# A hybrid decoder layer with expert retrieval: the dense expert loop's second stage with 512 moving columns, waits of single tiles, and 44 gathered expert rows traced later

## The chip, the core and the metric

The kernel runs on one core of a Trainium2 chip. Times are device microseconds (us) of one execution, from the first to the last instruction on the core plus what lies around it. Before the change the median of 3 runs is 2199.97 us (2193.77 to 2200.79). One further execution was taken with the profiler; all rows below are from it.

## What is computed

One layer of a decoder serves 512 prompt tokens (with 16 learned tokens in front) and 32 sample tokens, 1024 wide, all in float32. The first half (projection, a recurrence called RWKV-7, windowed attention, an output projection) gives the residual `x`. The second half is the retrieval of experts, and the change is about that part:

```python
def peer(h, lp):                                   # h = rmsnorm(x): [tokens, 1024]
    q = (hb @ w_query).reshape(n, 8, 2, 128)       # 8 heads, two half keys
    s = jnp.einsum('thcd,cnd->thcn', q, sub_keys)  # scores against 2 x 128 keys
    s1, i1 = lax.top_k(s[:, :, 0], 16)
    s2, i2 = lax.top_k(s[:, :, 1], 16)
    top, sel = lax.top_k(s1 + s2 (all 256 pairs), 16)
    idx = i1 * 128 + i2 at sel                     # 128 experts of 16384 for each token
    gate = softmax(top)
    pre = jnp.einsum('td,tkd->tk', hb, eu[idx])    # dot with row u of each expert
    act = gelu(pre) * gate
    return jnp.einsum('tk,tkd->td', act, ev[idx])  # weighted sum of rows v
# x = x + peer(rmsnorm(x)); y = rmsnorm(x) * final_norm_g
```

The expert tables `eu` and `ev` hold 16384 rows of 4 KB each, 64 MB apiece.

## The kernel before, in words

**Two ways to the experts.** The 512 prompt tokens are four tiles of 128. Tiles 0 and 3 and the samples *gather*: for each of the 128 picks (32 for the samples) one indirect DMA, issued by GpSimd (line 1032, `rows` inside `experts`), fetches one table row for each of 128 partitions, 512 KB, into one of five buffers `gat`. VectorE then takes a dot product (rows of `eu`) or adds the weighted row to the sum (rows of `ev`, tiles `x`); all VectorE instructions are recorded under line 126. That makes 256 gathers for a tile and 64 for the samples, 576 in all.

Tiles 1 and 2, 256 tokens, are done *densely*: every one of the 16384 experts is computed for all 256 tokens, and the weights of the experts that a token did not pick are zero. The table is cut into 128 blocks of 128 experts. Each block has these steps:

- `block_in` loads 128 rows of `eu` and of `ev`, transposes the `eu` rows on TensorE, and splits both into a high part in the fp32r format and a low part, the remainder (`uH`, `uL`, `vH`, `vL`; the split of `v` runs on ScalarE and GpSimd, line 1453).
- `block_u` multiplies with the tokens (`dhH`, `dhL`): 24 products of 256 columns (lines 1460 to 1463); then gelu, the gate, and a split of the result into `aH` and `aL`.
- `block_v` adds the block's part of the output into four PSUM tiles `acc`, which stay there through all 128 blocks: for each eighth of the 1024 output columns a slice of `vH` or `vL` is the weight operand and the activations are the moving operand, 256 columns; three products each (high with high, low with high, high with low, lines 1477 to 1479), 24 in all.

The result is transposed (output columns in the partitions, tokens along the row), so at the end `acc` is copied to `oT`, transposed in 16 pieces, added to the residual and normalised (`finish`).

**The stages in time.** In the *front* come the projections, the recurrences (`recur`), the attentions (`attend`) and the selections (`rest`) of all tiles; by 430 us gathers of tile 0 run beside it, and later those of the samples. Its buffers lie in the pools `sb` and `pp`. When it closes, the pools `dn` and `dp` take the same memory. First the normalised tokens come back from DRAM (line 1421, `hscr`), are transposed (1426) and split (`dhH`, `dhL`). Then `gates` builds, in 32 steps, the table of gate values by one-hot compares on VectorE; then comes the dense loop. Tile 3's selection (`late`) and its gathers run beside the dense loop.

**What sets the order.** The gathers are steps of generators in a list `side`; `beside(n)` traces the next n of them (fractions add up). `AHEAD` steps are traced ahead of the gates, then `RATE_G` = 0.8 for each gate step and `RATE_D` = 3 for each dense block; after the last block `beside(1000)` traces what is left. `issue_after` says behind which instruction such a step may be issued. The order on each engine is then fixed, before the kernel runs, by a list scheduler that follows a model of the timeline. Each engine works through its list in order.

A pool's memory that is handed from one pool to the next is guarded by waits: without an argument the first users of the new pool wait until the old pool as a whole is released; with `reuse_waits="tile"` each new tile waits only for the old tiles whose bytes it takes.

Of the kernel before, what the change touches and what calls it, by code (L numbers as in the profile page):

```python
# [11 lines left out]
F32 = mybir.dt.float32  # L12
# [3 lines left out]
OP = mybir.AluOpType  # L16
AX = mybir.AxisListType
PSUM = bass.MemoryType.PSUM
# [14 lines left out]
LAG = 2  # L33
WST = 3
UV = 5
AHEAD = 280
RATE_G = 0.8
RATE_D = 3.0
LATE = 2
# [74 lines left out]
def hymba_step(ctx, tc, x_prompt, x_sample, cache_k, cache_v, state_wkv, state_shift, meta, norm1_g, w_in, mu, w0,  # L114
# [3 lines left out]
    A, G, T, DM = nc.scalar, nc.gpsimd, nc.tensor, nc.sync  # L118
# [11 lines left out]
    V = V()  # L130
    uid = [0]

    def _t(pool, tag, bufs, shape, dt=F32):
        uid[0] += 1
        return pool.tile(list(shape), dt, tag=tag, name=f"{tag}_{uid[0]}", bufs=bufs)
# [13 lines left out]
    fr = ctx.enter_context(ExitStack())  # L149
# [15 lines left out]
    ident = p0.tile([128, 128], F32, name="ident")  # L165
# [79 lines left out]
    def beside(n):  # L245

        due[0] += n
        while side and due[0] >= 1.0:
            due[0] -= 1.0
            if next(side[0], None) is None:  # L250
                side.pop(0)
        due[0] = min(due[0], 1.0)
# [804 lines left out]
    def finish(x2, y, rows, dst, gf, kind="F"):  # L1057

        rms(x2[:rows], y[:rows], rows, gf, kind)
        DM.dma_start(dst, y[:rows])  # L1060

    def final_g(t):
        G.dma_start(t, fin_g.partition_broadcast(128))
        return t
# [96 lines left out]
    with ExitStack() as px:  # L1161
# [36 lines left out]
        def transposed(h, half, rows):  # L1198
            p = jps().rearrange("p (a b) -> p a b", a=4)
            for j in range(4):  # L1200
                k = 4 * half + j
                transpose(p[:, j, 0:rows], h[:rows, k * 128:(k + 1) * 128])
            return p
# [30 lines left out]
        for half in range(2):  # L1234
            p = transposed(hS, half, 72)
# [41 lines left out]
            project(blk, wt, ws, jps(), lambda k: [t[:, k, :] for t in hA], NA, _t(pj, "own", 2, [128, NA]),  # L1277
                    _t(pj, "po", 3, [128, NA]), 0)

    sb = fr.enter_context(tc.tile_pool(name="sb", bufs=1))  # L1280
    pp = fr.enter_context(tc.tile_pool(name="pp", bufs=1, space=PSUM))
    def meta_wkv():
        r = rwkv_prep(40, 16)
        wkv_local(r)
        meta_state(r)
# [119 lines left out]


    ND = 256
    dn = ctx.enter_context(tc.tile_pool(name="dn", bufs=1))
    dp = ctx.enter_context(tc.tile_pool(name="dp", bufs=1, space=PSUM))

    def dt_(tag, bufs, shape, dt=F32):
        return _t(dn, tag, bufs, shape, dt)

    def dps():
        return _t(dp, "w", 4, [128, 512])
# [3 lines left out]
    for i in range(2):  # L1419
        hn = dt_("uv", UV, [128, 2, D])[:, 0]  # L1420
        DM.dma_start(hn, hscr[1 + i])
        for half in range(2):
            p = dps().rearrange("p (a b) -> p a b", a=4)
            for j in range(4):
                k = 4 * half + j
                T.transpose(p[:, j, :], hn[:, 128 * k:128 * k + 128], ident)
            o = hH[:, 4 * half:4 * half + 4, 128 * i:128 * i + 128]
            A.copy(o, p)
            V.tensor_tensor(hL[:, 4 * half:4 * half + 4, 128 * i:128 * i + 128], p, o.bitcast(F32), OP.subtract)

    acc = [dp.tile([128, 2, ND], F32, name=f"acc{c}", bufs=1) for c in range(4)]
    euv = eu[0].rearrange("(i j) d -> i j d", j=128)
    evv = ev[0].rearrange("(i j) d -> i j d", j=128)

# [36 lines left out]

    def block_v(j, x):
        vH, vL, aH, aL = x
        for d in range(8):
            o = acc[d // 2][:, d % 2, :]
            ds_ = slice(128 * d, 128 * d + 128)
            T.matmul(o, vH[:, ds_], aH, start=(j == 0 and d % 2 == 0), stop=False, skip_group_check=True)  # L1477
            T.matmul(o, vH[:, ds_], aL, start=False, stop=False, skip_group_check=True)  # L1478
            T.matmul(o, vL[:, ds_], aH, start=False, stop=(j == 127), skip_group_check=True)  # L1479

    gA, gB = dt_("gA", 1, [128, 32, 128]), dn.tile([128, 64, 128], F32, name="gB")
    sg = [None]
# [69 lines left out]

    for n in range(AHEAD):
        with tc.issue_after(marks[gather_mark[0]]):
# [20 lines left out]
    for j in range(128):  # L1575
        nxt, mark = None, last
        if j < 127:
            nxt, last = block_u(ins.pop(j + 1), gate_of(j + 1))
        if j < 126:
            ins[j + 2], sub = block_in(j + 2)  # L1580
        block_v(j, mid)
        mid = nxt
        for _ in range(LATE):
            next(more, None)
        with tc.issue_after(mark), tc.issue_after(sub):
            beside(RATE_D)
    oT = gB[:, 0:16, :].rearrange("p a b -> p (a b)").rearrange("p (a b) -> p a b", b=ND)
    for c in range(4):
        A.copy(oT[:, 2 * c:2 * c + 2, :], acc[c])
    gfd = final_g(dt_("uv", UV, [128, 2, D])[:, 0])  # L1590
    for i in range(2):
        xy = dt_("uv", UV, [128, 2, D])
        x2, y = xy[:, 0], xy[:, 1]
        DM.dma_start(x2, xscr[1 + i])
        for half in range(2):
            p = dps()
            for q in range(4):
                k = 4 * half + q
                T.transpose(p[:, 128 * q:128 * q + 128], oT[:, k, 128 * i:128 * i + 128], ident)
            xs_ = x2[:, 512 * half:512 * half + 512]  # L1600
            V.tensor_tensor(xs_, xs_, p, OP.add)
        finish(x2, y, 128, y_p[0, 128 * (i + 1):128 * (i + 1) + 128, :], gfd, "E")
    beside(1000)

# [27 lines left out]
```

## Time and profile before

| | profiled execution before |
|---|---|
| device time of this execution | 2204.76 us |
| span on the core | 2203.0 us |
| mean granted clock of TensorE (1 is 2.4 GHz) | 0.867 |
| TensorE busy | 1839.1 us, 83% |
| VectorE busy | 1690.4 us, 77% |
| GpSimd busy | 1249.2 us, 57% |
| ScalarE busy | 867.3 us, 39% |
| moved by all DMA | 569.51 MB, mean 259 GB/s |

In the rows PE is TensorE's products and PEld its loads of weights, DVE is VectorE, ACT ScalarE, POOL GpSimd, SPq the DMA queue of SyncE. A row of the timeline has the start in us, the duration in us, the engine, the line, the operation, output<-inputs by the program's names, the shape and a count; in square brackets stands how long the engine was idle before and what ended that. A row of a table of windows has the stretch in us, its length, the busy time of each engine with the number of instructions, the granted clock, the mean share of the DMA engines that was busy, and GB/s. The gathers' DMA time is not in GpSimd's busy time: that holds only the issuing.

### The profile page before, as it was taken

The numbers are of one execution on the slowest core, as the hardware profiler recorded it, in microseconds if no ns is written. First come the engines' busy times: TensorE is split into PE (matmuls) and PEld (weight loads), VectorE is DVE, ScalarE is ACT, GpSimd is POOL, SyncE is SP. The second block draws the span as 40 slices with busy tenths as digits, with TensorE's granted clock in tenths as the row PEclk, the third lists the DMA queues.
The fourth block names the chain that finished last, engine by engine and source line by source line (L and its number), as shares of the span: only waits on it lengthen the run. The fifth ranks groups of instructions, "written<-read, shape, count | busy, mean of one in ns | idle before, by whom it ended". The sixth has DMA issues, their size and how long they took to land.

```text
span 2203.0 us, 37197 instructions
## 1 busy us (share of the span) xinstructions
PE 1839.1 (83%) x13915; PEld 1716.0 (78%) x13915; DVE 1690.4 (77%) x3393; ACT 867.3 (39%) x1963; POOL 1249.2 (57%) x963
## 2 busy tenths in 40 slices
PE   5899975585759868996547897899999999999996
PEld 5888974473647747886446787899999999999995
DVE  5543436788788788799989879997778787787887
ACT  6554422211224313323169634334444444444443
POOL 0110103878784676565624546867667776767774
PEclk9999996556755659898778999999999999999998
DMA  7532473687786789996757887799899999999995
GB/s 222 157 101 84 122 191 102 208 288 248 230 273 199 231 273 318 285 317 222 243 163 242 299 313 239 270 326 340 334 330 331 342 326 336 335 325 343 325 330 178
DMA packets 310154, 569.51 MB, mean 259 GB/s; under 512 B 32787, under 2 KB 194565, under 8 KB 309830
## 3 DMA queue, kind: packets, MB, share of 16 engines
q0 software_dynamic: 84048, 305.70, 39.7%
q1 hardware_dynamic: 225926, 261.43, 36.6%
q8 instruction: 110, 1.80, 0.3%
q14 instruction: 70, 0.57, 0.1%
HBM read 543.07 MB, written 24.60 MB: 258 GB/s over the span
## 4 chain that ended last, share of the span: by engine, by line
PE 51%; DVE 22%; DMA 10%; issue 9%; POOL 5%; ACT 3%; SPq 0%; DVEq 0%; POOLq 0%; ACTq 0%
DVE gat L126 5%; PE acc L1478 5%; PE w L1460 5%; PE w L1461 5%; PE w L1463 5%; PE acc L1479 5%; PE acc L1477 5%; PE w L1446 4%; POOL gat L1032 4%; DVE x L126 4%; PE pD L218 3%; DMA gat<-in_expert_v_dram,ei 3%; PE ps L218 2%; DMA wst<-in_w_query_dram 2%; DMA gat<-in_expert_u_dram,ei 2%
## 5 line engine op out<-in xcount | busy, mean ns | idle before, releaser
L126 DVE SCALAR_TENSOR_TENSOR x<-gat,act,x 128x1024 f32<-128x1024 f32 x287 | 427.9, 1491 | 24.7 <-DMA gat<-in_expert_v_dram,ei 23.4
L1032 POOL DMA_INDIRECT gat<-in_expert_u_dram,ei x256 | 343.0, 1340 | 158.8 <-DVE pre L126 75.7
L1032 POOL DMA_INDIRECT gat<-in_expert_v_dram,ei x256 | 294.4, 1150 | 193.6 <-DVE x L126 73.1
L1453 POOL TENSOR_TENSOR vL<-uv,vH 128x1024 fp32r<-128x1024 f32 x128 | 322.5, 2519 | 56.1 <-ACT vH L1452 54.3
L1478 PE MATMUL acc<-aL,vH 128*128 128x256 f32 x1024 | 290.7, 289 | 17.2 <-DVE aL L126 17.1
L1479 PE MATMUL acc<-aH,vL 128*128 128x256 f32 x1024 | 289.3, 287 | 0.0
L1477 PE MATMUL acc<-aH,vH 128*128 128x256 f32 x1024 | 280.5, 295 | 5.3 <-ACT aH L1469 5.3
L1460 PE MATMUL w<-dhH,uH 128*128 128x256 f32 x1024 | 252.5, 284 | 0.2 <-ACT lsc L1548 0.2
L1461 PE MATMUL w<-dhL,uH 128*128 128x256 f32 x1024 | 251.6, 283 | 0.0
L126 DVE CUSTOM_DVE_ANT_0 gat<-gat,h 128x1024 f32<-128x1024 f32 x160 | 213.5, 1343 | 49.6 <-DMA gat<-in_expert_u_dram,ei 47.8
L1478 PEld LDWEIGHTS acc<-aL,vH 128*128 128x128 f32 x1024 | 200.6, 196 | 19.3 <-DVE aL L126 19.3
L126 DVE CUSTOM_DVE_ANT_0 gat<-gat,lx 128x1024 f32<-128x1024 f32 x128 | 214.4, 1686 | 0.0
L1452 ACT CAST vH<-uv 128x1024 fp32r<-128x1024 f32 x128 | 134.6, 1051 | 195.7 <-issue 131.8
L1479 PEld LDWEIGHTS acc<-aH,vL 128*128 128x128 f32 x1024 | 200.6, 196 | 0.0
L1460 PEld LDWEIGHTS w<-dhH,uH 128*128 128x128 f32 x1024 | 196.9, 192 | 0.5 <-ACT lsc L1548 0.4
L1461 PEld LDWEIGHTS w<-dhL,uH 128*128 128x128 f32 x1024 | 196.8, 192 | 0.1
L1477 PEld LDWEIGHTS acc<-aH,vH 128*128 128x128 f32 x1024 | 188.0, 193 | 6.0 <-ACT aH L1469 5.9
L126 DVE TENSOR_TENSOR uL<-w,uH 128x512 fp32r<-128x512 f32 x256 | 167.6, 681 | 3.0 <-ACT uH L1448 3.0
L126 DVE TENSOR_TENSOR w<-w,gl 128x128 f32<-128x128 f32 x128 | 50.5, 395 | 143.3 <-ACT w L1464 143.2
L1463 PE MATMUL w<-dhH,uL 128*128 128x256 f32 x1024 | 151.9, 287 | 2.8 <-DVE uL L126 2.8
L1448 ACT CAST uH<-w 128x512 fp32r<-128x512 f32 x256 | 139.1, 592 | 8.4 <-PE w L1446 3.0
L1446 PE MATMUL w<-ident,uv 128*128 128x128 f32 x1024 | 141.4, 273 | 0.0
(575 smaller groups left out, 4113.8 us busy)
## 6 DMA issues: line engine op xcount, KB each, us to landing
uv<-in_expert_u_dram SPq DMA_DIRECT2D x128, 512.0 KB, 4.5
uv<-in_expert_v_dram SPq DMA_DIRECT2D x128, 512.0 KB, 5.9
wst<-in_w_query_dram SPq DMA_DIRECT2D x48, 512.0 KB, 5.5
wst<-in_w_out_dram SPq DMA_DIRECT2D x24, 512.0 KB, 6.9
wst<-in_w_in_dram SPq DMA_DIRECT2D x20, 512.0 KB, 4.4
h2T<-in_w_in_dram SPq DMA_DIRECT2D x20, 512.0 KB, 4.1
gscr<-uv SPq DMA_DIRECT2D x10, 1024.0 KB, 6.5
gl<-gscr SPq DMA_DIRECT2D x16, 512.0 KB, 7.4
```

Of the source, the lines that this page charges most:

```text
L126: r = getattr(nc.vector, name)(*args, **kw)
L1032: G.indirect_dma_start(out=r, out_offset=None, in_=w[0], in_offset=bass.IndirectOffsetOnAxis(ap=ei[:, k:k + 1], axis=0))
L1446: T.transpose(p[:, q, :], un[:, 128 * k:128 * k + 128], ident)
L1448: A.copy(uH[:, ks, :], p)
L1452: A.copy(vH, vn)
L1453: G.tensor_tensor(vL, vn, vH.bitcast(F32), OP.subtract)
L1460: T.matmul(pre, uH[:, k, :], hH[:, k, :], start=(k == 0), stop=False)
L1461: T.matmul(pre, uH[:, k, :], hL[:, k, :], start=False, stop=False)
L1463: T.matmul(pre, uL[:, k, :], hH[:, k, :], start=False, stop=(k == 7))
L1477: T.matmul(o, vH[:, ds_], aH, start=(j == 0 and d % 2 == 0), stop=False, skip_group_check=True)
L1478: T.matmul(o, vH[:, ds_], aL, start=False, stop=False, skip_group_check=True)
L1479: T.matmul(o, vL[:, ds_], aH, start=False, stop=(j == 127), skip_group_check=True)
```

## The change

The edit has three parts. `AHEAD` is 236 instead of 280, so 44 gather steps that were traced ahead of the gates are traced beside gates and dense blocks. The pools `sb`, `pp`, `dn` and `dp` get `reuse_waits="tile"`. And `block_v` swaps its operands: a slice of 128 tokens of `aH` or `aL` is the weight operand, and 512 columns of `vH` or `vL` move; for each of three pairs, two halves of the tokens and two halves of the columns that makes 12 products. `acc` then holds tokens in the partitions, and the copies to `oT` and the transposes at the end are dropped.

```diff
-AHEAD = 280
+AHEAD = 236
...
-    sb = fr.enter_context(tc.tile_pool(name="sb", bufs=1))
-    pp = fr.enter_context(tc.tile_pool(name="pp", bufs=1, space=PSUM))
+    sb = fr.enter_context(tc.tile_pool(name="sb", bufs=1, reuse_waits="tile"))
+    pp = fr.enter_context(tc.tile_pool(name="pp", bufs=1, space=PSUM, reuse_waits="tile"))
...
-    dn = ctx.enter_context(tc.tile_pool(name="dn", bufs=1))
-    dp = ctx.enter_context(tc.tile_pool(name="dp", bufs=1, space=PSUM))
+    dn = ctx.enter_context(tc.tile_pool(name="dn", bufs=1, reuse_waits="tile"))
+    dp = ctx.enter_context(tc.tile_pool(name="dp", bufs=1, space=PSUM, reuse_waits="tile"))
...
-    acc = [dp.tile([128, 2, ND], F32, name=f"acc{c}", bufs=1) for c in range(4)]
+    acc = [dp.tile([128, 512], F32, name=f"acc{c}", bufs=1) for c in range(4)]
...
     def block_v(j, x):
         vH, vL, aH, aL = x
-        for d in range(8):
-            o = acc[d // 2][:, d % 2, :]
-            ds_ = slice(128 * d, 128 * d + 128)
-            T.matmul(o, vH[:, ds_], aH, start=(j == 0 and d % 2 == 0), stop=False, skip_group_check=True)
-            T.matmul(o, vH[:, ds_], aL, start=False, stop=False, skip_group_check=True)
-            T.matmul(o, vL[:, ds_], aH, start=False, stop=(j == 127), skip_group_check=True)
+        for n, (a, v) in enumerate(((aH, vH), (aH, vL), (aL, vH))):
+            for i in range(2):
+                for c in range(2):
+                    T.matmul(acc[2 * i + c], a[:, 128 * i:128 * i + 128], v[:, 512 * c:512 * c + 512],
+                             start=(j == 0 and n == 0), stop=(j == 127 and n == 2))
...
-    oT = gB[:, 0:16, :].rearrange("p a b -> p (a b)").rearrange("p (a b) -> p a b", b=ND)
-    for c in range(4):
-        A.copy(oT[:, 2 * c:2 * c + 2, :], acc[c])
...
         for half in range(2):
-            p = dps()
-            for q in range(4):
-                k = 4 * half + q
-                T.transpose(p[:, 128 * q:128 * q + 128], oT[:, k, 128 * i:128 * i + 128], ident)
             xs_ = x2[:, 512 * half:512 * half + 512]
-            V.tensor_tensor(xs_, xs_, p, OP.add)
+            V.tensor_tensor(xs_, xs_, acc[2 * i + half], OP.add)
```

**What moves on GpSimd, at the end.** GpSimd's list before, from the last but one dense block's split of `v` (`vL`) on; `gat` rows are gathers of tile 3, and the load of `final_norm_g` belongs to that tile's output.

```order
L1453 TENSOR_TENSOR vL_21325<-uv_21305,vH_21324 128x1024
L1032 DMA gat_18624<-in_expert_v_dram,ei_11_105 128x1024
L1032 DMA gat_18627<-in_expert_v_dram,ei_11_105 128x1024
L1032 DMA gat_18709<-in_expert_v_dram,ei_11_105 128x1024
L1453 TENSOR_TENSOR vL_21404<-uv_21384,vH_21403 128x1024
L1032 DMA gat_18712<-in_expert_v_dram,ei_11_105 128x1024
L1032 DMA gat_18715<-in_expert_v_dram,ei_11_105 128x1024
L1063 DMA gat_18800<-in_final_norm_g_dram 128x1024
```

The same place now:

```order
L1453 TENSOR_TENSOR vL_19837<-uv_19817,vH_19836 128x1024
L1032 DMA gat_17260<-in_expert_v_dram,ei_11_105 128x1024
L1032 DMA gat_17330<-in_expert_v_dram,ei_11_105 128x1024
L1032 DMA gat_17333<-in_expert_v_dram,ei_11_105 128x1024
L1453 TENSOR_TENSOR vL_19904<-uv_19884,vH_19903 128x1024
L1032 DMA gat_17336<-in_expert_v_dram,ei_11_105 128x1024
L1032 DMA gat_17406<-in_expert_v_dram,ei_11_105 128x1024
...
L1032 DMA gat_18550<-in_expert_v_dram,ei_11_105 128x1024
L1032 DMA gat_18553<-in_expert_v_dram,ei_11_105 128x1024
L1063 DMA gat_18559<-in_final_norm_g_dram 128x1024
```

Behind the last block's split stand 2 gathers before and 48 now (of which four are shown). Ahead of the first block's split stand 306 before and 261 now, and between the first and the last split 268 and 267.

**What moves on VectorE, late in the front.** The list before, in the selections of the second tile of the dense part (`MAX`, `hl`, `dsel`); the `ISA` rows on `gat` and `pre` are the dots of gathered rows, and `ax<-pC,sD` are the last two steps of the attention of tile 3.

```order
L126 TENSOR_TENSOR ax_7785<-pC_7947,sD_7938 128x128
L126 TENSOR_TENSOR ax_7785<-pC_7960,sD_7938 128x128
L126 MAX vals_7107<-sco_1488_7046 128x8
L126 ISA gat_8871,pre_8833<-gat_8871,h_1981_8828 128x1024
L126 ISA pre_8833 128x1
L126 TENSOR_TENSOR dsel_18_112<-dsel_18_112,sR_7042 128x32
L126 MAX vals_7107<-sco_1488_7046 128x8 x2
L126 TENSOR_REDUCE dsel_16_110<-ce_7031 128x32
L126 ISA gat_8874,pre_8833<-gat_8874,h_1981_8828 128x1024
```

In the changed list no row of a gather stands in this stretch; the attention's last steps stand at its very end, behind the last selection and just ahead of the dense part's first split (`dhL`):

```order
L126 TENSOR_TENSOR ce_7301<-iota_86,hl_7291 128x512
L126 TENSOR_SCALAR sD_7927<-sD_7924 128x4
L126 TENSOR_TENSOR sD_7934<-sD_7927,snk 128x4
L126 TENSOR_REDUCE dsel_17_111<-ce_7301 128x32
L126 TENSOR_TENSOR sD_7929<-sD_7929,sD_7934 128x4
L126 RECIPROCAL sD_7938<-sD_7929 128x4
L126 TENSOR_TENSOR ax_7785<-pC_7947,sD_7938 128x128
L126 TENSOR_TENSOR ax_7785<-pC_7960,sD_7938 128x128
L126 TENSOR_TENSOR dhL<-w_8003,dhH 128x4x128
L126 TENSOR_TENSOR dhL<-w_8010,dhH 128x4x128
```

The attention of tile 3 moved back by more than 80 instructions, and VectorE has nothing between it and the dense part.

**What moves on TensorE, in a dense block.** The first six products of one block's second stage before (moving operand first, then the weights), of 24:

```order
L1477 MATMUL acc_8033<-aH_9994,vH_9928 128x256
L1478 MATMUL acc_8033<-aL_9995,vH_9928 128x256
L1479 MATMUL acc_8033<-aH_9994,vL_9929 128x256
L1477 MATMUL acc_8033<-aH_9994,vH_9928 128x256
L1478 MATMUL acc_8033<-aL_9995,vH_9928 128x256
L1479 MATMUL acc_8033<-aH_9994,vL_9929 128x256
```

The whole second stage of a block now:

```order
L1477 MATMUL acc_8033<-vH_9792,aH_9858 128x512
L1477 MATMUL acc_8034<-vH_9792,aH_9858 128x512
L1477 MATMUL acc_8035<-vH_9792,aH_9858 128x512
L1477 MATMUL acc_8036<-vH_9792,aH_9858 128x512
L1477 MATMUL acc_8033<-vL_9793,aH_9858 128x512
L1477 MATMUL acc_8034<-vL_9793,aH_9858 128x512
L1477 MATMUL acc_8035<-vL_9793,aH_9858 128x512
L1477 MATMUL acc_8036<-vL_9793,aH_9858 128x512
L1477 MATMUL acc_8033<-vH_9792,aL_9859 128x512
L1477 MATMUL acc_8034<-vH_9792,aL_9859 128x512
L1477 MATMUL acc_8035<-vH_9792,aL_9859 128x512
L1477 MATMUL acc_8036<-vH_9792,aL_9859 128x512
```

Twelve products stand where 24 stood; the low part of the activations, `aL`, is read by the ninth product and not by the second.

## Rows read from the trace of the kernel before

**Rows 1.** The page's head: the span, and busy time of each engine.

```profile
span 2203.0 us, 37197 instructions
...
PE 1839.1 (83%) x13915; PEld 1716.0 (78%) x13915; DVE 1690.4 (77%) x3393; ACT 867.3 (39%) x1963; POOL 1249.2 (57%) x963
```

**Rows 2.** Table of windows: stretch, its length, busy time (instructions) of each engine.

```profile
core 0: us, PE busy (x) PEld busy (x) DVE busy (x) ACT busy (x) POOL busy (x), PEclk, DMA share, GB/s
262.00:372.00 110.00, 75.60 (x554) 67.85 (x553) 56.34 (x298) 25.13 (x73) 25.66 (x45) 0.86 0.60 166
948.00:1111.00 163.00, 106.71 (x806) 96.62 (x805) 156.96 (x586) 39.55 (x116) 101.02 (x113) 0.83 0.77 245
...
1247.00:1469.00 222.00, 193.53 (x1484) 187.36 (x1483) 195.08 (x462) 84.51 (x167) 136.77 (x106) 0.95 0.84 293
1469.00:2151.00 682.00, 682.00 (x5771) 682.00 (x5770) 544.41 (x821) 287.48 (x517) 493.29 (x315) 1.00 0.92 332
```

**Rows 3.** The same for line 1477 alone: PE and PEld, clock, DMA.

```profile
1469.00:2151.00 682.00, 228.95 (x824) 151.63 (x824) 1.00 0.92 332
```

**Rows 4.** The same for line 1032, the gathers: POOL, clock, DMA.

```profile
948.00:1111.00 163.00, 43.88 (x42) 0.83 0.77 245
430.00:470.00 40.00, 30.09 (x25) 0.50 0.92 316
```

**Rows 5.** The same for the tiles gat: PE, PEld, DVE, ACT, POOL.

```profile
948.00:1111.00 163.00, 0.00 (x0) 0.00 (x0) 54.71 (x43) 1.15 (x2) 44.47 (x43) 0.83 0.77 245
```

**Rows 6.** Timeline, the end of the dense loop and the last gather.

```profile
2179.97 1.16 POOL L1032 DMA_INDIRECT gat<-in_expert_v_dram,ei  x1 [0.30 <-issue]
...
2184.18 0.41 PE L1479 MATMUL acc<-aH,vL 128*128 128x256 f32 x1
...
2184.39 2.25 PE L1599 MATMUL w<-ident,gB 128*128 128x128 f32 x16
...
2184.63 0.59 ACT L1589 COPY gB<-acc 128x512 f32<-128x512 f32 x1 [0.48 <-PE acc L1479]
2186.76 1.28 DVE L126 SCALAR_TENSOR_TENSOR x<-gat,act,x 128x1024 f32<-128x1024 f32 x1 [0.93 <-DMA gat<-in_expert_v_dram,ei]
```

**Rows 7.** Timeline, the first tile: its first weight load and last selection.

```profile
262.59 0.38 SPq L892 DMA_DIRECT2D wst<-in_w_out_dram  x1
...
368.72 0.69 DVE L126 TENSOR_REDUCE res<-ce 128x32 f32<-128x512 f32 x1 [1.44 <-POOL ce L1011]
```

**Rows 8.** Timeline of TensorE: products of 256, then of 314 columns.

```profile
259.48 0.46 PE L218 MATMUL pD<-gat,wst 128*128 128x314 f32 x2
...
261.23 0.45 PE L218 MATMUL pD<-gat,wst 128*128 128x314 f32 x2
...
1701.31 0.28 PE L1479 MATMUL acc<-aH,vL 128*128 128x256 f32 x1
...
1703.70 0.28 PE L1478 MATMUL acc<-aL,vH 128*128 128x256 f32 x1
```

**Rows 9.** Timeline, from the front's last selection to the gates.

```profile
1109.94 0.69 DVE L126 TENSOR_REDUCE dsel<-ce 128x32 f32<-128x512 f32 x1 [1.44 <-POOL ce L1011]
1110.69 0.82 SPq L1421 DMA_DIRECT2D uv<-hscr  x2
...
1114.57 3.65 PE L1426 MATMUL w<-ident,uv 128*128 128x128 f32 x16 [33.62 <-DMA uv<-hscr]
...
1116.36 0.69 DVE L126 TENSOR_TENSOR dhL<-w,dhH 128x512 fp32r<-128x512 f32 x1 [5.73 <-ACT dhH L1428]
...
1120.24 1.89 DVE L126 TENSOR_TENSOR uH<-vL,aH 128x1024 f32<-128x1024 bf16 x1
```

**Rows 10.** Timeline, the last normalisations of tiles 1 and 2.

```profile
2190.93 1.04 ACT L195 ACTIVATE uv<-uv 128x1024 f32<-128x1024 f32 x1
...
2196.05 1.28 DVE L126 SCALAR_TENSOR_TENSOR uv<-uv,sE,uv 128x1024 f32<-128x1024 f32 x1
```

**Rows 11.** VectorE's adds of gathered rows, 1469 to 2151: count, busy, mean ns.

```profile
L126 DVE SCALAR_TENSOR_TENSOR x<-gat,act,x 128x1024 f32<-128x1024 f32 x114 | 181.2, 1589 | 0.4
```

## The prediction

> **What bounds the kernel now.** The page comes first: TensorE is busy for 83% of the span, VectorE for 77%, GpSimd for 57% [rows 1], so the stages have to be read apart. A table of the busy time by stretch does that [rows 2]. In 1469-2151 us TensorE is busy for all 682 us at a granted clock of 1.00 (the 2.4 GHz level), and the transfers run at 332 GB/s. The first product of the dense loop's second stage stands there 824 times [rows 3], 8 to a block, so 103 of the 128 blocks take 682 / 103 = 6.62 us each, bound by TensorE. In 948-1111 us it is VectorE: 157.0 of 163 us. There the front's last selections, its last recurrence and 42 gathers [rows 4] share that engine, and everything that VectorE does on gathered rows takes 54.7 us [rows 5]. The end is read from the timeline: the last dense product starts at 2184.18, the last gather is issued at 2179.97 and its sum runs from 2186.76 to 2188.04 [rows 6]. The two strands end together; neither has a tail today.
>
> **Part 1, the place of 44 gathers.** AHEAD goes from 280 to 236. On GpSimd and VectorE the order is word for word the old one up to the 236th gather (in use at 948 us); after it no gather is left before the gates. The order of GpSimd also tells where they go: before its first dense block stand 261 gathers instead of 306, between the first and the last block 267 instead of 268, and behind the last block's split 48 instead of 2. So the blocks carry what they carried, and the 46 form a tail with no dense work beside it.
>
> What the front gives back: 157.0 - 54.7 = 102.3 us of VectorE work remain in the 163 us. Full packing would save 163 - 102 = 61 us. The other end comes from the first tile, which goes through the same projection and selection with hardly a gather beside it: from its first weight load at 262.59 to its last selection at 369.4 are 107 us [rows 7], with VectorE busy for about half of them (56.3 of 110 us, [rows 2]). Selections wait there for GpSimd (1.44 us before the last reduction, [rows 7]). In the changed stretch the recurrence and the tile before fill some of those waits. At three quarters busy the stretch takes 102 / 0.75 = 136 us and the saving is 27; I take 83%, nearer to the full row than to the half one because two strands share the engine: 123 us, a saving of **40**. The loads of projection weights, which now lie among gathers, will find free queues, but they only feed this strand and are within the 107 us.
>
> What the tail costs: 46 gathers at the pace of gathers with nothing else on the queues. The row for that is 430-470 us: 25 issues in 40 us at a DMA share of 0.92 [rows 4], 1.6 us each. VectorE's add of 1.28 us [rows 6] is under that, so transfers set the pace. 46 x 1.6 = **+74**; at 1.5 (a full share) 69, at 1.75 80. Nothing covers it: all that stands beside it are the outputs of two tiles.
>
> **Part 2, wider products.** A block's second stage has 24 products of 256 columns now and 12 of 512 afterwards: the same 6144 columns, half the instructions and half the weight loads. The weight loads lie beside products already, so only the spacing counts. In the steady stretch 20 products of 256 columns take 1703.70 - 1701.31 = 2.39 us, 119.5 ns each; in the front 12 of 314 columns take 261.23 - 259.48 = 1.75 us, 145.8 ns [rows 8]. If what exceeds one column per 2.4 GHz clock (119.5 - 106.7 = 12.8 ns) is a fixed price, 512 columns take 213.3 + 12.8 = 226 ns; the line through the two rows (0.453 ns per column) gives 235.5; in proportion it is 239. I take 231, midway between the first two. Saving per block: 12 x (2 x 119.5 - 231) = 0.096 us, over 103 blocks **-10**; ends 0 (239) and 12 x (239 - 226) x 103 = -16. No other unknown sits here: the new order of the three products needs aL only after eight of them instead of one, which loosens a wait and adds none, and vL comes from a block prepared two blocks earlier.
>
> The rows put 12.8 ns on top of the columns. The Trainium skill (TensorE: Matmul & The Clock Gate, "Wait - 56ns, not 53.3ns?") states that warm products follow each other after N / 2.4 GHz plus about 2.5 ns whatever N is; the row of 256 columns, 119.5 ns, is 10 ns over that rule. By the rule 512 columns would take 215.8 ns and this part would give 12 x (239 - 215.8) x 103 = 29 us; the sum goes by the rows, and the rule's result is a rival below.
>
> **Part 3, waits of single tiles.** Between front and gates VectorE idles for 5.73 us until 1116.36, because the two loads of hscr are issued only at 1110.69, when the last reduction of the front's pools (it starts at 1109.94) is done, and TensorE starts on them at 1114.57 [rows 9]. Afterwards these loads wait for single tiles instead. But the order on VectorE puts the third attention tile's last steps just ahead of the gates, and the loads wait for two of its products; their flight (1110.69 to 1114.57, 3.9 us) is still mostly open. **-2**, ends -6 and 0. At the front's own start the first load behind the pool needs the same six stores as before, as data: 0.
>
> **Part 4, the close.** Four copies of acc (at most 0.6 us of ScalarE each) and 16 transposes (2.25 us from 2184.39, [rows 6]) go. They lie beside the last gathers now and would lie beside the tail: 0. But tiles 1 and 2 will be finished long before the last sum, so the last normalisation no longer shares ScalarE with theirs: two squares of 1.04 us, and their sums of 1.28 us, which stand behind it now [rows 10]. About **-4**, ends -6 and 0. What comes late next is the 48th gather's flight and one tile's output.
>
> **The sum**: 2203.0 - 40 + 74 - 10 - 2 - 4 = 2221 us of span. The profiled execution took 2204.76, 1.8 more than its span, and 4.8 more than the median of the three runs, 2199.97. So 2221 + 1.8 - 4.8 = 2218 for a median.
>
> **Rivals.**
> (a) *VectorE packs the front fully*: the stretch of 948-1111 shrinks to its 102 us of work, -61 instead of -40, and the kernel ends faster with the wide products at their best: 2218 - 21 - 6 = 2191. For it: VectorE is busy 96% there today, so its queue finds work nearly always. Against it: what fills the waits today is largely the gathers that go, and the first tile without them filled half. It decides from a front saving of about 60 us on, with the tail at 69 to 74.
> (b) *The fixed price falls to the rule's 2.5 ns*: -29 instead of -10, 2199, no difference. Against it: neither row, at 256 or 314 columns, shows that spacing.
> (c) *The dense stage doesn't get faster*: at 6.5 us a block the transfers (share 0.92 at 6.62, [rows 2]) or VectorE would hold it. A block now carries two gathered rows; VectorE spends 544.4 / 103 = 5.3 us on one, because adds that take 1.28 us alone take 1.589 in the mean beside GpSimd [rows 11]. With the front at its low end of 27: 2218 + 10 + 13 = 2241.
> (d) *The tail is not there*, since faster hardware than the order supposes lets gathers run ahead: it can't be, as the gathers behind the last block stand behind it on GpSimd in order.
>
> **Chances.** Forecast 0.57, (a) 0.15, (b) 0.13, (c) 0.15. A measurement of this kernel tells about 0.3% from no change, 2193.4 to 2206.6 us. Faster: (a) and a little of the forecast's lower side, 0.18. Same: (b) and the forecast's lower edge, 0.20. Slower: the rest of the forecast and (c), 0.62. The forecast's own range is 2203 to 2233 (front 27 to 50, pace 1.5 to 1.75); the range with the rivals in it 2186 to 2242.
>
> **What would show it.** The gates' first compare on VectorE stands near 1080 us instead of 1120 [rows 9], and the dense loop starts near 1207 instead of 1247 (the bound of its first row in [rows 2]). In the steady stretch the products of 512 columns start every 226 to 236 ns and a block takes 6.5 us. TensorE falls silent some 75 us before the end, and in that tail only gathers and adds run, 1.6 us apart, at a DMA share over 0.9. The forecast is wrong if the tail runs under 1.3 us a gather, if the front shrinks by over 55 us, or if blocks take under 6.4 us.

## The result, and the profile after

The changed kernel takes 2235.44 us (median of 4 runs, 2227.62 to 2237.04) against 2200.38 us for the kernel before beside it: a ratio of 1.0163, 95% interval 1.0130 to 1.0197. It is slower by 35 us where 18 were forecast: the direction was right, but the forecast was about half of what came, and 2235 us lies 2 us above the upper end of its range.

The page's head after (answers to [rows 1]):

```profile
span 2234.2 us, 34116 instructions
...
PE 1820.0 (81%) x12363; PEld 1627.5 (73%) x12363; DVE 1694.1 (76%) x3393; ACT 866.1 (39%) x1962; POOL 1269.1 (57%) x963
```

The stretches of the changed kernel, a line each: the end of the front, the gates, the first and the steady part of the dense loop, and two pieces of the tail (answers to [rows 2]; columns as there):

```profile
947.10:1078.70 131.60, 101.23 (x794) 92.82 (x794) 98.84 (x499) 38.49 (x109) 40.71 (x69) 0.85 0.44 130
1078.70:1206.20 127.50, 81.56 (x543) 75.16 (x542) 119.61 (x161) 116.09 (x342) 54.02 (x25) 0.90 0.68 218
1206.20:1428.00 221.80, 195.71 (x1290) 178.96 (x1291) 186.93 (x462) 82.87 (x163) 134.08 (x106) 0.95 0.84 298
1428.00:2110.00 682.00, 675.37 (x4543) 620.64 (x4542) 553.65 (x861) 293.05 (x530) 512.58 (x316) 1.00 0.91 332
2143.00:2163.00 20.00, 0.21 (x1) 0.00 (x0) 17.04 (x18) 6.28 (x17) 11.55 (x11) 0.59 0.92 323
2163.00:2218.00 55.00, 0.00 (x0) 0.00 (x0) 42.70 (x34) 0.00 (x0) 44.64 (x34) 0.50 0.89 309
```

The reader is to see three things. The front's last stretch is shorter, but VectorE is busy for only 98.84 of 131.60 us there, 75%; 10.2 of the idle us stand at its very end. The steady part of the loop is bound by TensorE as before. And after 2143 us TensorE does nothing for 91 us, while gathered rows come and are added one after the other.

Where the time went is read from seven marks that both traces have: VectorE's copy `XT` at 952.03 before and 947.11 after (3.6 of the 4.9 us between them stand ahead of 940 us, up to where VectorE's order is the same), the first split `dhL`, the first product of the dense loop, the first of the last block, the end of the last split `vL`, the end of the last add of a gathered row, and the end.

| stretch | before | after | difference | forecast |
|---|---|---|---|---|
| start to the `XT` mark | 952.0 | 947.1 | -4.9 | 0 |
| to the first `dhL` | 164.3 | 131.6 | -32.7 | -42 (front -40, handover -2) |
| gates, to the first dense product | 124.4 | 127.5 | +3.1 | 0 |
| dense loop, to its last block | 930.2 | 919.7 | -10.5 | -10 |
| to the end of the last split | 6.8 | 9.9 | +3.1 | 0 |
| gathers behind it, to the last add | 10.3 | 90.2 | +79.9 | +74 |
| to the end | 15.0 | 8.1 | -6.9 | -4 |
| sum | 2203.0 | 2234.2 | +31.2 | +18 |

The handover from the front to the dense part, timeline after (answers to [rows 9]):

```profile
1068.19 0.29 DVE L126 TENSOR_TENSOR ax<-pC,sD 128x128 f32<-128x128 f32 x1 [3.21 <-PE pC L816]
...
1070.51 0.34 SPq L1354 DMA_DIRECT2D yscr<-dx  x1
1071.60 0.58 ACT L1359 COPY gn<-pC 64x512 f32<-64x512 f32 x1 [1.12 <-PE pC L184]
1072.20 0.65 SPq L1360 DMA_DIRECT2D out_dram<-gn  x1
1072.96 1.03 SPq L1421 DMA_DIRECT2D uv<-hscr  x2
...
1076.95 3.65 PE L1426 MATMUL w<-ident,uv 128*128 128x128 f32 x16 [5.39 <-DMA uv<-hscr]
...
1078.69 0.69 DVE L126 TENSOR_TENSOR dhL<-w,dhH 128x512 fp32r<-128x512 f32 x1 [10.21 <-ACT dhH L1428]
...
1082.46 3.61 DVE L126 TENSOR_TENSOR uH<-vL,aH 128x1024 f32<-128x1024 bf16 x2
```

VectorE idles 10.21 us ahead of `dhL`, where it was 5.73. On SyncE's queue the loads of `hscr` come right behind two stores of the front's end, the second of which (line 1360) waits for ScalarE's copy that starts at 1071.60.

The second stage's products, in groups of four, in the steady stretch (answers to [rows 8]):

```profile
1700.36 1.08 PE L1477 MATMUL acc<-vL,aH 128*128 128x512 f32 x4
1701.28 1.07 PE L1477 MATMUL acc<-vH,aL 128*128 128x512 f32 x4
1702.19 0.28 PE L1460 MATMUL w<-dhH,uH 128*128 128x256 f32 x1
```

Four products of 512 columns take 1701.28 - 1700.36 = 0.92 us, 230 ns each; 231 was taken. The Trainium skill (TensorE: Matmul & The Clock Gate, "Wait - 56ns, not 53.3ns?") gives N / 2.4 GHz plus about 2.5 ns, an estimate of 215.8 ns for 512 columns; the measurement is 14 ns over it and decides.

The end of the tail, timeline after (answers to [rows 6]):

```profile
2133.19 2.70 POOL L1453 TENSOR_TENSOR vL<-uv,vH 128x1024 fp32r<-128x1024 f32 x1
2136.04 1.75 POOL L1032 DMA_INDIRECT gat<-in_expert_v_dram,ei  x1 [0.15 <-issue]
...
2215.46 1.28 DVE L126 SCALAR_TENSOR_TENSOR x<-gat,act,x 128x1024 f32<-128x1024 f32 x1 [0.48 <-DMA gat<-in_expert_v_dram,ei]
...
2217.86 1.48 POOL L1032 DMA_INDIRECT gat<-in_expert_v_dram,ei  x1 [0.30 <-issue]
...
2224.84 1.28 DVE L126 SCALAR_TENSOR_TENSOR x<-gat,act,x 128x1024 f32<-128x1024 f32 x1 [1.09 <-DMA gat<-in_expert_v_dram,ei]
2226.15 1.06 ACT L195 ACTIVATE gat<-x 128x1024 f32<-128x1024 f32 x1 [74.80 <-DVE x L126]
...
2230.39 0.33 SPq L1060 DMA_DIRECT2D out_dram<-gat  x1
```

From 2136.04 to 2217.86 there are 47 steps from one gather to the next, 1.74 us each in the mean. The pace is not even: the first 25 us, beside the last sums and the outputs of tiles 1 and 2, are slower, and from 2161.09 on a step takes 1.67 us. There almost every issue starts 1.1 us behind the end of the add that frees its buffer, five gathers back: the add of 2215.46 ends at 2216.74, and the gather that takes its buffer starts at 2217.86. So it is the round trip of a buffer that holds the pace. GpSimd's list looks full there (44.64 us of issuing and some 0.3 us between two issues in 55 us), but its issues last from 0.9 to 1.9 us, each as a rule up to 0.8 us behind the add that frees the next one's buffer: waiting is in them. ScalarE has been idle for 74.80 us when it comes to the last normalisation.

### The profile page after: what moved, and what is told of

Same layout as the page of the kernel before. It is cut to its first block, busy times and chain, and to the rows that moved or that the text cites. A ratio compares the mean times of both kernels' runs of the same rounds, so it can differ in the third digit from the quotient of the medians.

```text
span 2234.2 us, 34116 instructions
## 1 busy us (share of the span) xinstructions
PE 1820.0 (81%) x12363; PEld 1627.5 (73%) x12363; DVE 1694.1 (76%) x3393; ACT 866.1 (39%) x1962; POOL 1269.1 (57%) x963
## 3 DMA queue, kind: packets, MB, share of 16 engines
q8 instruction: 98, 1.61, 0.3%
## 5 line engine op out<-in xcount | busy, mean ns | idle before, releaser
L1032 POOL DMA_INDIRECT gat<-in_expert_v_dram,ei x256 | 346.0, 1352 | 223.1 <-DVE x L126 127.4
L126 DVE SCALAR_TENSOR_TENSOR x<-gat,act,x 128x1024 f32<-128x1024 f32 x287 | 440.2, 1534 | 36.6 <-DMA gat<-in_expert_v_dram,ei 35.1
L1032 POOL DMA_INDIRECT gat<-in_expert_u_dram,ei x256 | 337.9, 1320 | 160.2 <-DVE pre L126 87.5
L126 DVE CUSTOM_DVE_ANT_0 gat<-gat,lx 128x1024 f32<-128x1024 f32 x128 | 191.7, 1512 | 3.5 <-DMA gat<-in_expert_u_dram,ei 3.5
L1477 PE MATMUL acc<-vH,aH 128*128 128x512 f32 x512 | 155.1, 420 | 11.2 <-ACT aH L1469 11.2
L1477 PE MATMUL acc<-vH,aL 128*128 128x512 f32 x512 | 139.7, 394 | 8.6 <-DVE aL L126 8.6
L1463 PEld LDWEIGHTS w<-dhH,uL 128*128 128x128 f32 x1024 | 136.4, 193 | 9.1 <-DVE uL L126 7.9
L1477 PE MATMUL acc<-vL,aH 128*128 128x512 f32 x512 | 140.6, 396 | 0.0
L952 PE MATMUL pD<-h2T,wst 128*128 128x128 f32 (+1 forms) x768 | 107.6, 294 | 15.6 <-DMA wst<-in_w_query_dram 15.4
L1477 PEld LDWEIGHTS acc<-vH,aL 128*128 128x128 f32 x512 | 96.2, 189 | 32.1 <-DVE aL L126 11.4
```

The lines of the kernel that those rows point to most:

```text
L126: r = getattr(nc.vector, name)(*args, **kw)
L952: T.matmul(p[:, 0:tot], wt[:, k, :], h2T[:, k, :], start=(k == 0), stop=(k == 7))
L1032: G.indirect_dma_start(out=r, out_offset=None, in_=w[0], in_offset=bass.IndirectOffsetOnAxis(ap=ei[:, k:k + 1], axis=0))
L1463: T.matmul(pre, uL[:, k, :], hH[:, k, :], start=False, stop=(k == 7))
L1477: T.matmul(acc[2 * i + c], a[:, 128 * i:128 * i + 128], v[:, 512 * c:512 * c + 512], start=(j == 0 and n == 0), stop=(j == 127 and n == 2))
```

## The experiments

The kernel before was timed again beside the experiments: 2199.98 us beside the first four, 2197.91 beside the next four, 2197.03 beside the last three. A single execution of one kernel varies by some 10 us either way, much of it before the `XT` mark (last section), so stretches are compared from the mark on.

**E1: the changed kernel with AHEAD at 280.**

```diff
-AHEAD = 236
+AHEAD = 280
```

> The changed kernel with AHEAD back at 280; the wide second stage and the tile-wise waits stay. Theory (the moved gathers alone make the loss; the parts add): without the tail of 46 gathers (80 us at 1.74 us each in the changed kernel's trace) and with the front's 42 us back, only the wide products' 10 us remain: about 2190 us, ratio to before 0.995, and blocks of 6.50 us. Rival 1 (the tile-wise waits cost time, since they put the third attention last and the loads of hscr behind its stores): 2196 us, ratio 0.998, with VectorE idle for about 10 us before the gates. Rival 2 (the dense loop's gain is given back at its end): 2200 us, ratio 1.000, the last add of a gathered row as late as before.

Measured: 2183.74 us, ratio 0.9935 (0.9906 to 0.9965). That is faster than both kernels. From the mark to the first `dhL` 159.4 us, and VectorE is not idle before it; the last add ends at 2177.5. So the moved gathers alone turn a gain of 16 us into a loss of 35. Neither rival held; the theory's 0.995 lies inside the interval.

**E2: the wide second stage alone.** The kernel before with the changed `acc`, `block_v` and end.

> The kernel before with the 512-column second stage alone (and without the copies and transposes at the end); AHEAD 280, whole-pool waits. Theory: blocks fall from 6.62 to 6.50 us, 10 to 12 us over the loop, 2190 us, ratio 0.995. Rival (gathers on GpSimd then end the loop, which keep their pace): blocks of 6.50 us, but the last add of a gathered row is as late as before and the time stays at 2197 to 2200, ratio 0.999 to 1.000.

Measured: 2192.62 us, ratio 0.9963 (0.9939 to 0.9987). The loop from its first to its last block takes 920.4 us against 930.2: the wide products give 10 us.

**E3: the tile-wise waits alone.** The kernel before with `reuse_waits="tile"` on the four pools.

> The kernel before with the tile-wise waits of the four pools alone. Theory (they are worth little while gathers fill the front): 2197 to 2201 us, ratio 0.999 to 1.000, VectorE idle before the gates between 2 and 6 us. Rival (the waits let the attention of tile 3 slide back and cost the 4 us that the changed kernel's trace has more at the handover): 2204 to 2206 us, ratio 1.002 to 1.003, VectorE idle for about 10 us there.

Measured: 2189.43 us, ratio 0.9950 (0.9927 to 0.9974); faster than either the theory or the rival had it. Timeline of E3 at the handover:

```profile
1074.25 1.03 SPq L1421 DMA_DIRECT2D uv<-hscr  x2
...
1103.09 0.69 DVE L126 TENSOR_REDUCE dsel<-ce 128x32 f32<-128x512 f32 x1 [1.44 <-POOL ce L1011]
1103.70 1.88 DVE L126 TENSOR_TENSOR dhL<-w,dhH 128x512 fp32r<-128x512 f32 x3
```

The loads are issued 29 us ahead of VectorE's last reduction and no longer right behind it; VectorE goes from the selection to the split in one go. From the mark to `dhL` it takes 157.8 us, 6.6 less, of which 5.7 are the idle time at the handover (5.7 to 0). Of the rest of the 11 us the trace has 1.2 in the gates and 2.4 in the loop; that these come from the waits is not shown. So at AHEAD = 280 the waits pay. At 236 they can bring little at the handover, because VectorE has no selections left to do while the loads fly: it idles there for 10.2 us with them and for 11.1 without (E4). The waits alone were not run at 236.

**E4: AHEAD = 236 alone.**

```diff
-AHEAD = 280
+AHEAD = 236
```

> The kernel before with AHEAD = 236 alone: 256-column second stage, whole-pool waits. Theory (the move makes the loss, the parts add): the changed kernel's time and the 10 us of the wide products on top, 2245 us, ratio 1.020; if the handover keeps its old 5.7 us, 4 us less, 2241. Rival (the tile-wise waits or the wide products bring part of the loss): 2230 us or less, ratio 1.014.

Measured: 2249.08 us, ratio 1.0225 (1.0183 to 1.0267), with the theory's 1.020 inside. The loss belongs to the move. VectorE idles for 11.1 us at the handover here too, without any tile-wise wait, so the longer handover comes from the order that goes with 236.

**E5 and E6: AHEAD = 260 and 300 in the changed kernel.**

```diff
-AHEAD = 236
+AHEAD = 260
...
-AHEAD = 236
+AHEAD = 300
```

> The changed kernel with AHEAD = 260, so that 20 gathers move and not 44; by the order 27 gathers stand behind the last dense block's split. Theory (each gather moved costs 1.74 us in the tail and gives back 0.96 us in the front): from 2190 at 280 a tail of 23 more gathers, +40, and -20 in the front: 2209 us, ratio 1.004. Rival (the loss is a fixed one of the new order): near the changed kernel's 2235, ratio over 1.012.

> The changed kernel with AHEAD = 300: 14 more gathers ahead of the dense loop than at 280 (320 against 306 by the order), 4 behind the last split in both. Theory (TensorE sets the dense loop, so gathers taken out of it give nothing back): the front grows by 14 to 20 x 0.96 us, 2203 to 2209 us, ratio 1.002 to 1.004. Rival (gathers set the end of the loop): blocks get faster by as much, and the time stays at 2190, ratio 0.995.

Measured: 2191.78 us at 260, ratio 0.9996 (0.9958 to 1.0033), below both expectations; 2205.88 us at 300, 1.0057 (1.0026 to 1.0087), inside the theory's times. The stretch from the mark to `dhL`, table of windows, of E5 and then of E6:

```profile
951.20:1084.30 133.10, 101.97 (x792) 92.33 (x790) 129.20 (x532) 40.94 (x117) 70.05 (x92) 0.87 0.72 228
```

```profile
936.70:1121.50 184.80, 103.90 (x792) 92.69 (x790) 178.07 (x605) 44.11 (x120) 125.22 (x133) 0.78 0.83 275
```

At 260 VectorE is busy for 129.2 of 133.1 us, 97%: 21 gathers lie in this stretch, and it is only 1.5 us longer than without them at 236. From 260 to 280 and on to 300 it grows by 26 and 25 us for 20 gathers each, 1.3 us a gather. The 0.96 us a gather of the expectation were a mean over unlike pieces. At 300 the loop's first to last block takes 908.1 us against 924.4 in E1, which gives 16 of the 25 us back; so the theory's reason (nothing given back) did not hold though its time did, and neither did the rival (all given back).

**E7: two stores on another queue.**

```diff
-    DM.dma_start(yscr, yT3)
+    G.dma_start(yscr, yT3)
...
-    DM.dma_start(wkv_p[0, 0].rearrange("h i j -> i h j"), wp.rearrange("p (h j) -> p h j", h=8))
+    G.dma_start(wkv_p[0, 0].rearrange("h i j -> i h j"), wp.rearrange("p (h j) -> p h j", h=8))
```

> The changed kernel with two stores of the front's end (yscr and the recurrence's final state) on GpSimd's queue and not on SyncE's. Theory (SyncE's list holds the loads of hscr back: they stand behind these two stores, which wait for ScalarE's copies): the loads are issued 1.5 to 3 us earlier against VectorE's last step of the front, and VectorE's idle time before the gates falls from 10.2 to 7 to 8.5 us. Rival (the loads wait for the memory that ScalarE's last copies use): the idle time stays at 10 us.

Measured in one execution: 2233.66 us. Timeline of E7:

```profile
1067.58 2.90 SPq L1421 DMA_DIRECT2D uv<-hscr  x2
...
1072.69 0.60 POOL L1354 DMA_DIRECT2D yscr<-dx  x1 [9.54 <-ACT dx L1352]
...
1073.86 1.97 PE L1426 MATMUL w<-ident,uv 128*128 128x128 f32 x16 [0.67 <-ACT gn L1359]
...
1075.17 0.69 DVE L126 TENSOR_TENSOR dhL<-w,dhH 128x512 fp32r<-128x512 f32 x1 [4.77 <-ACT dhH L1428]
```

Both loads are issued before VectorE's last step of the front has ended (at 1070.4) instead of 4.5 us behind it, and the idle time is 4.77 us instead of 10.21. SyncE's list held them back; the effect is larger than expected. What is left no longer waits for the loads: TensorE's transposes (line 1426) now start behind ScalarE's copy `gn`, the last of the front.

**E8 and E10: a sixth buffer for tile 3's rows of `expert_v`.** A dense tile that is free by then (`ly`) joins the rotation.

```diff
+    def more_gat(k):
+        return _t(dn, "ly", 1, [128, 8, 128]).rearrange("p a b -> p (a b)") if k % 6 == 5 else gat()
...
-                r = gat()
+                r = more_gat(k) if w is ev and ei is pl1[0] else gat()
```

> The changed kernel with a sixth buffer in the rotation for the gathered rows of expert_v of tile 3 (a tile of the dense part that is free by then). Theory (the transfers set the pace of the tail, at a DMA share of 0.9): still 1.65 to 1.75 us a gather and a span within 4 us of 2234. Rival (the round trip of a buffer sets it: 6.0 us from issue to landing, then the wait for the add and the add, 8.7 us for five buffers): 8.7 / 6 = 1.45 us a gather, 46 x 0.29 = 13 us less.

> The changed kernel with the sixth buffer in tile 3's rotation again, timed. Of the 28 us in its one trace 16 stood before 930 us, where nothing differs, and 10 in the tail. Theory (the sixth buffer works in the tail alone): 46 gathers x 0.13 us and two gathers fewer, 2223 to 2227 us, ratio 1.011 to 1.013. Rival (the front gains with it): 2208 us again, ratio 1.004.

Measured: 2208.19 us in the one execution of E8; timed in E10 2223.84 us, ratio 1.0137 (1.0085 to 1.0189). The tail in E10, table of windows:

```profile
2144.00:2164.00 20.00, 0.00 (x0) 0.00 (x0) 17.95 (x17) 4.81 (x15) 13.96 (x11) 0.50 0.94 333
2164.00:2204.00 40.00, 0.00 (x0) 0.00 (x0) 34.82 (x28) 0.00 (x0) 31.52 (x28) 0.50 0.97 351
```

Over the whole tail the pace is 1.61 us (both traces) instead of 1.74, between the two expectations. But the first 20 us hold 11 gathers as in the changed kernel; behind them, from 2163.17 to the last issue at 2204.05, 28 steps take 1.46 us each instead of 1.67, at a DMA share of 0.97 instead of 0.89. That is the rival's 1.45: there the round trip of a buffer holds the pace, and each issue still starts 1.1 us behind the add that frees its buffer, now six gathers back. At a share of 0.97 the transfers have little left to give. E10's expectation, which went by the mean of E8's trace, held. The timed difference to the changed kernel, 2235.4 - 2223.8 = 12 us, is for the most part the tail's: from the last split to the last add 80.7 us (E10, two gathers fewer) against 90.2.

**E9: AHEAD = 248 in the changed kernel.**

```diff
-AHEAD = 236
+AHEAD = 248
```

> The changed kernel with AHEAD = 248; by the order 275 gathers stand ahead of the dense loop (261 at 236, 287 at 260) and 39 behind the last split (48 and 27). Theory (in the last stretch of the front VectorE has room for some 20 gathers beside its other work, a chain through ScalarE and TensorE setting the end, so these cost nothing there): from the 952 us mark to the dense part's first split 131 to 134 us, as at 236 (131.6) and at 260 (133.1), and VectorE over 85% busy; the time falls only by the tail's 9 gathers, 16 us, to 2219. Rival (each gather costs its 1.3 us of VectorE there): 131.6 + 14 x 1.3 = 150 us, and no gain over the changed kernel, 2235.

Measured: 2201.45 us, ratio 1.0040 (1.0008 to 1.0071), below both expectations. The stretch from the mark to `dhL`, table of windows:

```profile
934.90:1059.30 124.40, 98.59 (x784) 90.16 (x784) 110.56 (x519) 36.97 (x106) 53.51 (x80) 0.87 0.59 183
```

With 10 gathers in it the stretch is the shortest of all, 124.4 us, 7.2 less than with none; 4.8 of that is the handover, where VectorE idles for 5.4 us and not 10.2. The tail is 76.1 us. That up to some 20 gathers cost nothing in the front is not borne out. From the mark to the end of VectorE's last step of the front, that is without the handover, it takes 121.4 us with none (236), 119.0 with 10 (248) and 133.2 with 21 (260): about ten are free, and the next eleven cost 1.3 us each, as further ones do. In the whole stretch this is hidden, because the idle time of the handover falls from 10.2 to 5.4 and to 0 us at the same time. What else the order of 248 does better than that of 236 was not taken apart.

**E11: AHEAD = 280 and the sixth buffer.** E1 with the edit of E8.

> The changed kernel with AHEAD = 280 and the sixth buffer. Theory (without a tail the buffers matter little, TensorE sets the blocks): within 4 us of the 2184 us without it, ratio 0.992 to 0.995. Rival (the gathers hold the end of the dense loop too): 2174 to 2178 us, ratio 0.989.

Measured: 2167.38 us (2167.08 to 2169.61), ratio 0.9877 (0.9828 to 0.9925): the fastest of all. The rival held, and by more than it said. GpSimd's waits for VectorE to free a buffer (`gat` for `x`: us, times, longest), from the loop's first product to the end of its 121st block, in E1 and then in E11:

```profile
POOL gat L1032 <- DVE x L126: 70.0, 33, 9.3
```

```profile
POOL gat L1035 <- DVE x L126: 40.4, 14, 9.3
```

Between first and last block the loop takes 906.0 us instead of 924.4. So even where TensorE is busy nearly all the time, the chain from GpSimd through a buffer to VectorE's add, beside which TensorE's next operand is made, set part of the loop. (The scheduler's order changes with the buffer too; what of the 18 us is order alone was not tested.)

From the `XT` mark to the end the profiled executions read: 236: 1287.1; 248: 1258.5; 260: 1249.4; 280: 1239.1; 300: 1249.6; with the sixth buffer 236: 1276.9 and 280: 1220.2 us.

## Why the prediction was right and wrong

By the marks the forecast's sum missed 13 us of span. The largest single miss is the handover from the front to the dense part, put at -2 and measured at +4.5; then come the tail's pace (+6) and two stretches put at nothing (+6). The sum's other terms came out near their size.

*That the 46 gathers form a tail with nothing beside them.* Right, and the cause of the loss: E1 and E4 differ from the changed kernel and the kernel before by this move alone, and it costs 49 us in the one pair (2249.1 against 2200.0) and 52 in the other (2235.4 against 2183.7).

*The tail's price, +74.* Mis-sized: +79.9. The step that failed here is the pace, 25 issues in 40 us and so 1.6 us each. The count of 25 took in an issue that began before the window. From start to start the same stretch gives 1.69 us:

```profile
430.77 0.95 POOL L1032 DMA_INDIRECT gat<-in_expert_u_dram,ei  x1 [0.30 <-issue]
...
469.67 0.95 POOL L1032 DMA_INDIRECT gat<-in_expert_u_dram,ei  x1 [0.30 <-issue]
```

These are 23 steps in 38.90 us, and 46 x 1.69 would have given 78. "Transfers set the pace" was wrong for five buffers: the round trip of a buffer did, at a DMA share of 0.89. With six it still did, at 1.46 us and a share of 0.97 (E10).

*The front's saving, -40.* Nearly right. To the end of its last step of the front VectorE takes 121.4 us from the mark where it took 158.6, 37.2 less, and it is busy for 98.8 of them: 81% packing, 83% was taken. What it waits for there (us, times, longest) is no single chain but the attention (`ax`), the selections (`vals`, `dsel`) and the recurrence (`Yl`):

```profile
DVE ax L126 <- PE pC L816: 5.3, 2, 3.2
DVE vals L126 <- ACT sco L959: 4.5, 3, 2.0
DVE Yl L126 <- PE pB L572: 4.0, 1, 4.0
DVE dsel L126 <- POOL ce L1011: 3.1, 3, 1.2
```

*The handover, -2.* This step failed, in its sign: VectorE waits 10.2 us ahead of `dhL` where it waited 5.7, +4.5. The prediction saw that the third attention's last steps stand just ahead of the gates, but not that the loads of `hscr` stand on SyncE behind two stores that wait for those steps' results. E7 shows this queue to be worth 5.4 us of idle time; the stretch to `dhL` is 3.9 us shorter there. The other 4.8 us come with the order, in which nothing is left for VectorE to do.

*What one saving for all 44 gathers hid.* The first 20 taken out (280 to 260) give 26.3 us, 1.3 each, all of VectorE's time on them. The last 24 give 1.5 us together: the first eleven of them (260 to 248) still give VectorE 1.3 us each, the rest had lain in its waits, and the handover's idle time takes 10.2 us back. In the tail each of the 44 costs 1.74 us. So no part of the move paid: even where a gather costs its full price in the front, that is less than its price in the tail.

*Wide products, -10.* Right in the mechanism: 230 ns a product, 10 us in the loop in E2. Rival (b), a fixed price that falls, is ruled out by the 230 ns; (c), no faster blocks, by the blocks' own times: from the 41st block on every group of eight takes 6.49 to 6.59 us a block, and 6.62 before (its last group 7.14). That the whole loop is shorter by just 10.5 us is in part luck: narrow products with the same move take 937.6 us (E4), 18 more than the changed kernel, and narrow ones with the tile-wise waits at 280 take 927.8 (E3), 3.4 more than E1. What lies outside the steady blocks moves by several us with the order of the gathers. Rival (a), full packing, did not come: 81% without gathers, 97% with 21 of them (E5).

*The close, -4.* -6.9: both dense tiles had long been finished, as said; no second normalisation shares ScalarE or the stores.

*What was costed at nothing.* The gates took 3.1 us more, as in all runs at AHEAD = 236 (127.5 to 128.3 against 124.4), and the last split came 3.1 us later against TensorE, which E4 does not show; neither was taken apart. Small, but of the same sign as the misses above: 6 for the pace, 3 for the front, 6.5 for the handover, 6 here, less 3 for the close and 5 before the mark, make the 13 us between +18 and +31. The remaining 4 us to the medians' 35 are within their spread.

## What to carry to other kernels

A filler that sits in the waits of a stretch is free there and costs its full price anywhere without cover: before moving it, price it at both places, piece by piece, and together with the waits that its absence opens. Read a pace from start to start and not by count over window, and ask whether buffers or transfers set it: one more buffer (E11 against E1, 16 us) was worth as much as wide products and tile-wise waits together (E1 against the kernel before, 16 us). A load behind a store on one queue waits for the store's data as well; look at each queue's list at the place where a stage hands over.

## What the hardware showed that was not expected

In the middle of the front the granted clock of TensorE rises earlier in some executions than in others, with no difference in the program there, and those executions are some 12 us shorter. The same 40 us in the trace before and in E8, table of windows:

```profile
680.00:700.00 20.00, 19.10 (x73) 14.80 (x72) 18.62 (x26) 9.53 (x16) 11.54 (x10) 0.50 0.58 172
700.00:720.00 20.00, 19.32 (x76) 15.46 (x75) 11.85 (x16) 3.56 (x8) 6.45 (x5) 0.50 0.47 151
```

```profile
680.00:700.00 20.00, 18.86 (x82) 14.32 (x80) 18.62 (x25) 10.60 (x18) 11.49 (x10) 0.60 0.59 178
700.00:720.00 20.00, 18.41 (x129) 15.55 (x127) 20.00 (x29) 6.81 (x16) 14.63 (x9) 0.92 0.63 191
```

TensorE is busy nearly throughout in both, before the rise too (19.10 and 18.86 of 20 us). From 700 us on it runs at the 1.2 GHz level (0.50) in the one and mostly at 2.4 GHz (0.92) in the other, and does 76 and 129 products. E6, E8 and E9 show the early rise, the ten other traces the late one; why it comes early in some is not shown. In E8 the `XT` mark stands at 929.2 us and in E10, the same kernel, at 943.3; that is 14 of the 16 us by which the single execution of E8 was faster than E10's median. Much of the spread of single executions is likely of this kind, but the executions without a trace cannot tell.
